# Three small moves in a decoder-layer kernel: late constants, a low weight part behind a scaling, a later first pooling

## The chip, the cores and the metric

The kernel runs on one core of one Trainium2 chip. A core has TensorE (PE: matrix multiplications, with PEld for its weight loads), VectorE (DVE), ScalarE (ACT), GpSimd (POOL) and SyncE (SP), each with its own instruction queue, worked off in order; SP here only issues DMA transfers, and POOL issues the gathers beside its own arithmetic. The metric is the device time of one execution in microseconds (us), lower is better.

## The reference, cut to what is computed

One step of a hybrid layer for a prompt of 512 tokens and 8 sampled tokens, with D = 1024, in float32:

```python
z = rms_norm(x, ln1_g) @ w_in            # u, q, keys and values of three sub-branches, gates
...
cmp_k, cmp_v, end = compress_kv(...)     # the paged cache pooled to one row per 16 tokens
o_c = softmax(q @ cmp_k - alibi) @ cmp_v # compressed blocks
sel = top blocks by the summed weights of o_c, gathered, attended
o_w = sliding window of 512 attended
attn = gates-weighted sum of the three
conv = pointwise(silu(layer_norm(depthwise conv, width 31)))
x = x + (sig(g_conv) * conv + sig(g_attn) * attn) @ w_out
x = x + relu(rms_norm(x) @ w_up)^2 @ w_down, then a last norm
```

The sampled tokens attend to a cache of 2048 tokens in pages of 128, which is read by index; the 16 best blocks of 64 tokens are chosen for each of them.

## The kernel before, in words

All 520 tokens stay on chip, transposed, as a high part hH and a low part hL of 8 slices of 128 channels. A float32 product is made of three products of rounded parts: high by high, low by high, high by low. `dense` (L437, L438, L439, with the accumulators psd) issues them slice by slice for two halves of the tokens, 256 and 264 columns, and remembers the last matmul of each half in the list `ends`. `wload` brings one block of 128 weight columns in two DMA pieces of 256 KB each (tile wraw, three buffers in turn), has ACT round each piece to the high part wh (L414) and lets DVE or POOL subtract to get the low part wl (L416). The first two loads and the seventh on go to POOL, the four between to DVE. SP issues the loads (L402); a load waits until the low part that used its buffer is done.

The start: SP loads the tokens xt (L234), the norm's weights and the first weights. `norm1` goes by a list written out by hand (NORDER): squares on ACT (L330), the root and a Newton step, the scaling of a block of tokens by DVE (L340, kept in the list `scaled`), transposes on PE (L348), high and low parts by ACT (L350) and DVE (L351). Ahead of the first transposes PE multiplies a block of ones by itself 20 times (L356). The first two weight blocks are asked for with `ins=scaled[1]`, which keeps their low parts behind the second scaling in issue order on an engine that has both, and makes no wait.

Then four head groups follow. `project(g)` makes queries, keys and values; for group 0 the queries are `ends[0..3]`, the keys `ends[4]` and `ends[5]`, the values `ends[6]` and `ends[7]`. ACT copies the results out (L569, L587), PE turns them for the outputs (L594, L600). Scores stand in PSUM (L681), DVE adds the distance term and finds the maximum (L645), ACT exponentiates (L649), PE turns the weights (L742) and multiplies by the values (L747). Between them run the pooling of the cache, the convolution's inputs and the taps of the convolution on DVE (L1109).

`pool_cache` gathers the cache's pages by index from POOL (L319, tile cg, four buffers), pools them by matmuls (L775 into psp, then L782) and passes the result through two small layers (L787 to L804). Its first pooling comes, in issue order, behind `ends[P_AT]`. After the last sample (CS_B = 7) it calls `conv_state`, which works on the old convolution rows (L1119 to L1131; PE L1124, DVE L1127 and L1128) and whose last DMA is kept as `UY["cs"]` (L1131). `sample_cmp` chooses the blocks: scores of the samples against the pooled keys (PE L825), a softmax with the table scb (DVE L829), a sum over heads with gsel (PE L837), a ranking with lt (DVE L859 to L863) and a mask spread by eb (PE L869, DVE L870). It begins with the loads of these four tables (L814 to L820).

What stands in the file is not yet the order of the engines. A scheduler lays all instructions out on a simulated timeline by priorities and expected ends, and each engine's queue is what comes out; `tc.issue_after` puts instructions behind another in that layout without a wait, `tc.add_manual_dep` with SYNC makes a real wait. So a constraint at one place can shift rows on all engines for a long stretch.

Of the kernel before, what the change touches and what calls it, by code (L numbers as in the profile page):

```python
# [13 lines left out]
OP = mybir.AluOpType  # L14
# [3 lines left out]
P = 128  # L18
# [41 lines left out]
WIN_E = lambda nc: nc.gpsimd  # L60
XF = False
LOW_D = 6
P_AT = 5
SQ_D, WARM, EARLY = (), 20, 2
NORDER = "q0 q1 s02 m0 m1 t0 t1 q2 q4 q3 s25 m4 m2 t4 m3 t2 t3"
PACK = 5000
# [1 line left out]
SYNC = mybir.DependencyInfo(mybir.DependencyClass.Sync, mybir.DependencyReason.DATA)  # L68
# [62 lines left out]
def hybrid_layer(ctx: ExitStack, tc: tile.TileContext, I, C, O):  # L131
    nc = tc.nc
# [11 lines left out]
    act, dve, pool, pe = nc.scalar, nc.vector, nc.gpsimd, nc.tensor  # L144

    def f32(ap):
        return ap.bitcast(F32)
# [235 lines left out]
    scaled = []  # L383
# [5 lines left out]
    LOW, loaded = [pool], []  # L389
    RAW = [wts, WR_B]  # L390

    def wfetch(w, pieces, r0=0, start=False):
        raws = []
        for h in range(2):
            if start:
                raw = once([P, KD // 2, P], f"wraw{pieces[0][0]}{h}")
            else:
                raw = RAW[0].tile([P, KD // 2, P], F32, name="wraw", tag="raw", bufs=RAW[1])
            o = 0
            for c, n in pieces:  # L400
                r = r0 + D // 2 * h
                nc.sync.dma_start(raw[:, :, o:o + n], w[r:r + D // 2, c:c + n].rearrange("(k p) c -> p k c", p=P))  # L402
                o += n
            raws.append(raw)
        return raws

    def wload(w, pieces, r0=0, low=None, ins=None):
        raws = early.pop(pieces[0][0], None) or wfetch(w, pieces, r0)
        o = sum(n for c, n in pieces)
        wh = wts.tile([P, KD, P], F32R, name="wh")  # L410
        wl = wts.tile([P, KD, P], F32R, name="wl")
        for h, raw in enumerate(raws):
            a, b = wh[:, KD // 2 * h:KD // 2 * h + KD // 2, :o], wl[:, KD // 2 * h:KD // 2 * h + KD // 2, :o]
            act.copy(a, raw[:, :, :o])  # L414
            with after(ins):
                (low or (dve if 2 <= len(loaded) < LOW_D else LOW[0])).tensor_tensor(b, raw[:, :, :o], f32(a), op=OP.subtract)  # L416
        loaded.append(wh)
        return wh, wl

    def after(ins):  # L420
        return tc.issue_after(ins.ins) if ins else nullcontext()

    def packed(makers, *ready_):
        with tc.high_priority(offset=PACK):
            for n, make in enumerate(makers):
                mm = make()
                for i in ready_ if n == 0 else ():
                    tc.add_manual_dep(mm.ins, i.ins.name, SYNC, reason="packed")
        return mm
# [329 lines left out]
    def pool_cache(pp):  # L759
        ps_ = psp if POOL_P else pst  # L760
        for b in range(NB):
# [4 lines left out]
            for rh in range(2):  # L766
                gs, gd = [], []
                for i in range(4):
                    g = pp.tile([P, 2, 512], F32, name="cg", bufs=CG_B)
                    gd.append(gather(cache_c, gic[:, b, i, rh:rh + 1], g))  # L770
                    gs.append(g)
                while len(ends) <= P_AT:
                    yield
                with after(ends[P_AT] if b + rh == 0 else None):
                    packed([lambda r=r, j=j, i=i: pe.matmul(po[32 * i:32 * i + 32, j], wpa[:, 2 * rh + r, j],  # L775
# [34 lines left out]

    def sample_cmp(bp, msk, oC):
        bt = lambda shape, name: bp.tile(shape, F32, name=name)
        gsel = bt([P, 2, 32], "gsel")
        nc.sync.dma_start(gsel, C["gsel"])  # L814
        eb = bt([32, NB, P], "eb")
        nc.sync.dma_start(eb, C["eb"])
        lt, eq, gt = bt([32, 30, 30], "lt"), bt([32, 15, 30], "eq"), bt([32, 15, 30], "gt")
        nc.sync.dma_start(lt, C["lt"])
        scb = bt([P, P], "scb")
        nc.sync.dma_start(scb, C["scb"])  # L820
        pc = bt([P, 2, P], "pcs")
        sv = bt([P, 2, 4], "sv")
        imp = bt([32, P], "imp")
# [32 lines left out]
        for n in (slice(0, 15), slice(15, 30)):  # L856
            a = sc[:, 1][:, None, :].to_broadcast([32, 15, 30])
# [504 lines left out]
    UY = {}  # L1362
# [291 lines left out]
```

## Time and profile before

| | |
|---|---|
| median of 3 runs | 1182.87 us (1182.01 to 1184.0) |
| the profiled execution, its own time | 1182.46 us |
| its span in the trace | 1180.7 us, so 1.76 us lie outside |
| mean granted clock of TensorE | 0.987 |
| PE busy | 1127.9 us, 96% |
| DVE busy | 749.8 us, 64% |
| ACT busy | 544.4 us, 46% |
| POOL busy | 250.4 us, 21% |

The busy shares are means over stages with different limits. In the 40 slices of the span PE is busy nine tenths or more from the fifteenth to the last but one, and seven to nine tenths before. The clock row shows what the throttle granted, 1.00 for the full 2.4 GHz and 0.50 for 1.2 GHz. A row of the timeline gives start, duration, engine, line, operation, output and input tiles and count, then in brackets the idle time before it and what ended it.

### The profile page before, as it was taken

Reading aid. Unit: us, or ns where it says so; the run is one execution under the profiler, and the core shown is the slowest. Engines: PE = TensorE matmul, PEld = TensorE weight load, DVE = VectorE, ACT = ScalarE, POOL = GpSimd, SP = SyncE. Lnnn points to the kernel's source line nnn. Section 1 sums busy time; section 2 is a strip of 40 time slices with the busy share of each in tenths; the row PEclk is TensorE's granted clock in tenths of the full one; section 3 lists DMA queues with packets and bytes.
Section 4 is the critical chain, followed back from the end, with each engine's and each line's share of the span. In section 5 each row is a group of like instructions: output and inputs, shape, how many; then the busy total and the mean of one; then the engine's idle time right before and its main releaser. Section 6 shows DMA issues by size and latency. Waiting matters only on the chain.

```text
span 1180.7 us, 24758 instructions
## 1 busy us (share of the span) xinstructions
PE 1127.9 (96%) x9755; PEld 1001.5 (85%) x9755; DVE 749.8 (64%) x1773; ACT 544.4 (46%) x1384; POOL 250.4 (21%) x284
## 2 busy tenths in 40 slices
PE   7899989899989899999999999999999999999996
PEld 7778867488668475788889889999999999999996
DVE  5441556939999778958959786556543543443476
ACT  5453463543554564566564464344431431432354
POOL 2345445546343122134221000000000000000012
PEclk8999989999999999999999999999999999999998
DMA  6746446428243855688984423333333333333353
GB/s 181 220 132 200 151 134 202 127 75 236 64 130 91 273 194 198 233 303 299 312 282 133 108 63 91 90 93 105 90 90 90 97 97 94 90 90 90 90 175 130
DMA packets 188366, 175.47 MB, mean 149 GB/s; under 512 B 35278, under 2 KB 171022, under 8 KB 182985
## 3 DMA queue, kind: packets, MB, share of 16 engines
q1 hardware_dynamic: 172472, 96.54, 28.6%
q0 software_dynamic: 15296, 76.55, 18.7%
q8 instruction: 77, 1.26, 0.4%
q10 hardware_dynamic: 480, 0.79, 0.2%
q14 instruction: 41, 0.33, 0.1%
HBM read 167.58 MB, written 14.80 MB: 154 GB/s over the span
## 4 chain that ended last, share of the span: by engine, by line
PE 77%; DVE 13%; DMA 3%; ACT 3%; issue 2%; POOL 1%; SPq 0%; DVEq 0%; ACTq 0%; POOLq 0%
PE psd L437 19%; PE psd L438 19%; PE psd L439 19%; DVE y L1109 5%; PE psx L936 3%; PE pss L681 2%; DMA cg<-in_cache_cmp_kv_dram,gic 2%; PE psp L775 2%; PE psy L951 2%; PE pso L747 2%; PE psy L940 2%; PE pst L742 2%; DVE pp L645 1%; DVE pp L731 1%; DVE pt L745 1%
## 5 line engine op out<-in xcount | busy, mean ns | idle before, releaser
L414 ACT CAST wh<-wraw 128x512 fp32r<-128x512 f32 x282 | 161.7, 616 | 289.9 <-PE psd L438 220.0
L437 PE MATMUL psd<-hH,wh 128*128 128x264 f32 (+2 forms) x848 | 249.4, 295 | 0.0
L439 PE MATMUL psd<-hH,wl 128*128 128x264 f32 (+2 forms) x848 | 245.7, 291 | 1.3 <-DVE wl L416 1.3
L438 PE MATMUL psd<-hL,wh 128*128 128x264 f32 (+2 forms) x848 | 245.4, 290 | 0.0
L416 DVE TENSOR_TENSOR wl<-wraw,wh 128x512 fp32r<-128x512 f32 (+1 forms) x230 | 155.4, 711 | 95.0 <-ACT wh L414 90.9
L1109 DVE SCALAR_TENSOR_TENSOR y<-u,cwT,y 128x512 f32<-128x512 f32 x240 | 197.7, 824 | 4.7
L437 PEld LDWEIGHTS psd<-hH,wh 128*128 128x128 f32 (+1 forms) x848 | 159.6, 189 | 8.8 <-issue 5.6
L438 PEld LDWEIGHTS psd<-hL,wh 128*128 128x128 f32 (+1 forms) x848 | 159.9, 189 | 6.6 <-issue 5.9
L439 PEld LDWEIGHTS psd<-hH,wl 128*128 128x128 f32 (+1 forms) x848 | 159.2, 188 | 6.5 <-issue 4.3
L437 PE MATMUL psd<-xgH,wh 128*128 128x264 f32 (+1 forms) x512 | 144.8, 283 | 0.0
L438 PE MATMUL psd<-aT,wh 128*128 128x264 f32 (+1 forms) x512 | 144.7, 283 | 0.0
L437 PE MATMUL psd<-aT,wh 128*128 128x264 f32 (+1 forms) x512 | 144.7, 283 | 0.0
L439 PE MATMUL psd<-aT,wl 128*128 128x264 f32 (+1 forms) x512 | 144.7, 283 | 0.0
L439 PE MATMUL psd<-xgH,wl 128*128 128x264 f32 (+1 forms) x512 | 144.5, 282 | 0.0
L438 PE MATMUL psd<-xgL,wh 128*128 128x264 f32 (+1 forms) x512 | 144.2, 282 | 0.0
L1593 POOL TENSOR_TENSOR attnT<-attnT,gfb 128x512 f32<-128x512 f32 (+1 forms) x8 | 10.5, 1330 | 533.5 <-DVE sqd L1588 533.5
L649 ACT ACTIVATE pp<-pp,st 128x128 f32<-128x128 f32 (+3 forms) x128 | 71.3, 557 | 84.5 <-DVE st L645 84.4
L438 PEld LDWEIGHTS psd<-xgL,wh 128*128 128x128 f32 x512 | 96.6, 189 | 0.0
L439 PEld LDWEIGHTS psd<-xgH,wl 128*128 128x128 f32 x512 | 96.5, 188 | 0.0
L437 PEld LDWEIGHTS psd<-aT,wh 128*128 128x128 f32 x512 | 96.3, 188 | 0.1
L437 PEld LDWEIGHTS psd<-xgH,wh 128*128 128x128 f32 x512 | 96.3, 188 | 0.0
L438 PEld LDWEIGHTS psd<-aT,wh 128*128 128x128 f32 x512 | 96.2, 188 | 0.0
(381 smaller groups left out, 2250.3 us busy)
## 6 DMA issues: line engine op xcount, KB each, us to landing
wraw<-in_w_in_dram SPq DMA_DIRECT2D x88, 256.0 KB, 4.7
wraw<-in_w_down_dram SPq DMA_DIRECT2D x80, 256.0 KB, 2.9
wraw<-in_w_up_dram SPq DMA_DIRECT2D x64, 256.0 KB, 2.9
sg<-in_state_win_kv_dram POOLq DMA_DIRECT2D x8, 1024.0 KB, 5.9
out_dram<-in_state_win_kv_dram SPq DMA_DIRECT2D x8, 1022.0 KB, 18.6
wraw<-in_w_in_dram SPq DMA_DIRECT2D x32, 128.0 KB, 2.6
wraw<-in_w_conv_pw_dram SPq DMA_DIRECT2D x16, 256.0 KB, 2.9
wraw<-in_w_out_dram SPq DMA_DIRECT2D x16, 256.0 KB, 3.1
```

The source lines that it names most:

```text
L414: act.copy(a, raw[:, :, :o])
L416: (low or (dve if 2 <= len(loaded) < LOW_D else LOW[0])).tensor_tensor(b, raw[:, :, :o], f32(a), op=OP.subtract)
L437: pe.matmul(ps[:n], wh[:, k, :n], aH[:, k, c], start=(k == 0), stop=False)
L438: pe.matmul(ps[:n], wh[:, k, :n], aL[:, k, c], start=False, stop=False)
L439: end = pe.matmul(ps[:n], wl[:, k, :n], aH[:, k, c], start=False, stop=(k == KD - 1))
L649: act.activation(ph, ph, AF.Exp, scale=-1.0, bias=st[:, 0, e, i:i + 1], accum_out=st[:, 1, e, i:i + 1])
L681: mms.append(lambda ps=ps, e=e, i=i, xi=xi, nk=nk: pe.matmul(ps, rq(e, i), KR[g, e, r][:, 32 - xi:32 + nk], start=True, stop=True))
L742: pe.transpose(ps[:, o:o + P], phs[e][i][:, P * j:P * j + P], ident)
L747: packed([lambda j=j, e=e: pe.matmul(po[64 * e:64 * e + 64, P * j:], vt[:, j, r], pts[e][:, off[j]:off[j] + P * (4 - j)], start=(r == 0 an ...
L775: packed([lambda r=r, j=j, i=i: pe.matmul(po[32 * i:32 * i + 32, j], wpa[:, 2 * rh + r, j], gs[i][:, r, 256 * j:256 * j + 256], start=(rh ...
L936: pe.transpose(ps[:, r], g[:, r, P * h:P * h + P], ident)
L1109: prev = dve.scalar_tensor_tensor(yk, u[:, w:w + NP_], cwT[:, k, w:w + 1], yk, op0=OP.mult, op1=OP.add)
```

## The change

It does three things. `P_AT` goes from 5 to 7, so that the first pooling stands behind the values' last matmul instead of the keys'. In `wload`, the first half's low part of a load with `ins` gets a real wait for the second scaling. And the loads of the four tables of `sample_cmp` are put behind `UY["cs"]` in issue order, and come as lt, scb, gsel, eb.

```diff
-P_AT = 5
+P_AT = 7
...
             act.copy(a, raw[:, :, :o])
             with after(ins):
-                (low or (dve if 2 <= len(loaded) < LOW_D else LOW[0])).tensor_tensor(b, raw[:, :, :o], f32(a), op=OP.subtract)
+                lo = (low or (dve if 2 <= len(loaded) < LOW_D else LOW[0])).tensor_tensor(b, raw[:, :, :o], f32(a), op=OP.subtract)
+            if ins and h == 0:
+                tc.add_manual_dep(lo.ins, ins.ins.name, SYNC, reason="scaled")
         loaded.append(wh)
...
     def sample_cmp(bp, msk, oC):
         bt = lambda shape, name: bp.tile(shape, F32, name=name)
+        hold_ = tc.issue_after(UY["cs"].ins)
+        hold_.__enter__()
+        lt, eq, gt = bt([32, 30, 30], "lt"), bt([32, 15, 30], "eq"), bt([32, 15, 30], "gt")
+        nc.sync.dma_start(lt, C["lt"])
+        scb = bt([P, P], "scb")
+        nc.sync.dma_start(scb, C["scb"])
         gsel = bt([P, 2, 32], "gsel")
         nc.sync.dma_start(gsel, C["gsel"])
         eb = bt([32, NB, P], "eb")
         nc.sync.dma_start(eb, C["eb"])
-        lt, eq, gt = bt([32, 30, 30], "lt"), bt([32, 15, 30], "eq"), bt([32, 15, 30], "gt")
-        nc.sync.dma_start(lt, C["lt"])
-        scb = bt([P, P], "scb")
-        nc.sync.dma_start(scb, C["scb"])
+        hold_.__exit__(None, None, None)
```

The same instructions stand on each engine in both programs, but not in the same order. From the file's line 416 on, the line numbers of the new program are 2 higher, behind the tables' loads 5 higher: L439, L440, L441 there are L437, L438, L439 here, L596 is L594, L647 is L645, L777 is L775, L1132 is L1127.

SP, the front of the queue, before:

```order
1 L814 DMA gsel_4937<-c_gsel_dram 128x64
2 L816 DMA eb_4939<-c_eb_dram 32x1024
3 L818 DMA lt_4941<-c_lt_dram 32x900
4 L820 DMA scb_4945<-c_scb_dram 128x128
5 L234 DMA xt0_89<-in_x_prompt_dram 128x1024
6 L234 DMA xt1_90<-in_x_prompt_dram 128x1024
7 L237 DMA g1b_94<-in_ln1_g_dram 128x1024
8 L234 DMA xt4_93<-in_x_sample_dram 8x1024
```

and in the change:

```order
1 L234 DMA xt0_89<-in_x_prompt_dram 128x1024
2 L234 DMA xt1_90<-in_x_prompt_dram 128x1024
3 L237 DMA g1b_94<-in_ln1_g_dram 128x1024
4 L234 DMA xt4_93<-in_x_sample_dram 8x1024
5 L239 DMA ident_95<-c_ident_dram 128x136
```

The four tables are gone from here and stand behind L1131's DMA, ahead of the window copies (L1380).

PE, the end of group 0's keys (psd rows of 128x264), before; psd rows of 128x256 that follow are the values:

```order
150 L437 MATMUL psd<-hH,wh 128x264
151 L438 MATMUL psd<-hL,wh 128x264
152 L439 MATMUL psd<-hH,wl 128x264
153 L775 MATMUL psp<-cg,wpa 32x256 x16
154 L594 MATMUL psj<-ident,qkv 128x128 x2
155 L437 MATMUL psd<-hH,wh 128x256
156 L438 MATMUL psd<-hL,wh 128x256
```

and in the change, at the same place and where the pooling now stands:

```order
152 L441 MATMUL psd<-hH,wl 128x264
153 L596 MATMUL psj<-ident,qkv 128x128 x2
154 L439 MATMUL psd<-hH,wh 128x256
155 L440 MATMUL psd<-hL,wh 128x256
...
206 L440 MATMUL psd<-hL,wh 128x256
207 L441 MATMUL psd<-hH,wl 128x256
208 L777 MATMUL psp<-cg,wpa 32x256 x2
209 L683 MATMUL pss<-qkv 128x384
210 L683 MATMUL pss<-ks,qkv 128x384
211 L777 MATMUL psp<-cg,wpa 32x256 x14
```

The pooling went from row 153 to rows 208 to 211, and the turning of the queries took its place. On POOL the two low parts of the first weight block changed places: the second half's comes first, the first half's, which has the new wait, second. From there to about 400 us every pooling stands 50 to 90 rows later on PE than before. In the stretch that ran from 310 to 335 us, 8 to 11 more conv taps (L1109) stand on DVE ahead of the same head's scores (L645); some 15 scores later the count is the same again.

DVE, the last pair of 128x512 scores (L645 with dist; "ISA st" reads the maximum) and the softmax of the block choice, before:

```order
742 L829 ISA pcs,sv<-psp,scb 128x128
743 L829 ISA sv 128x1
744 L745 COPY pt<-pst 128x512
745 L655 TENSOR_SCALAR st<-st 128x8
746 L656 RECIPROCAL st<-st 128x8
747 L645 ISA pp,st<-pss,dist 128x512
748 L645 ISA st 128x1
749 L657 TENSOR_TENSOR st<-st,gtok 128x8
750 L645 ISA pp,st<-pss,dist 128x512
751 L645 ISA st 128x1
752 L832 TENSOR_SCALAR sv<-sv 128x2
```

and in the change:

```order
739 L647 ISA pp,st<-pss,dist 128x512
740 L647 ISA st 128x1
741 L658 RECIPROCAL st<-st 128x8
742 L416 TENSOR_TENSOR wl<-wraw,wh 128x512
743 L1073 SCALAR_TENSOR_TENSOR u<-tb,ah 128x264
744 L747 COPY pt<-pst 128x384
745 L659 TENSOR_TENSOR st<-st,gtok 128x8
746 L1132 TENSOR_TENSOR tm<-psp,cwT 128x480
747 L657 TENSOR_SCALAR st<-st 128x8
748 L719 TENSOR_TENSOR pc<-pc,st 128x128 x2
749 L1133 TENSOR_REDUCE ys<-tm 128x4x4
750 L658 RECIPROCAL st<-st 128x8
```

A second low part stands between the two scores (row 738), another pair L1132 and L1133 at rows 752 and 754, and the two L834 (L829 before) at rows 759 and 761; before, all of these stood ahead of the pair. On PE 16 rows of L825 and two groups of L1124 come behind the last scores that stood ahead of them. From about 470 us on all engines have the same order in both programs.

## Rows read from the trace of the kernel before

**Rows 1.** Timeline, SP, the front of its queue: start, duration, engine, line.

```profile
0.75 0.40 SPq L814 DMA_DIRECT2D gsel<-c_gsel_dram  x1
...
2.60 0.91 SPq L234 DMA_DIRECT2D xt<-in_x_prompt_dram  x2
```

**Rows 2.** Timeline, start, ACT, DVE and PE; in brackets idle time and its releaser.

```profile
6.84 1.06 ACT L330 ACTIVATE sq<-xt 128x1024 f32<-128x1024 f32 x1 [4.59 <-DMA xt<-in_x_prompt_dram]
...
12.09 1.09 PE L348 MATMUL pst<-ident,xt 128*128 128x128 f32 x8 [3.42 <-DVE xt L340]
...
15.46 0.59 ACT L350 CAST hH<-pss 128x512 fp32r<-128x512 f32 x1 [0.32 <-PE pss L348]
...
16.31 0.59 ACT L350 CAST hH<-pss 128x512 fp32r<-128x512 f32 x1 [0.27 <-PE pss L348]
...
16.82 0.58 PE L438 MATMUL psd<-hL,wh 128*128 128x256 f32 x1
...
23.91 0.28 PE L438 MATMUL psd<-hL,wh 128*128 128x256 f32 x1
...
24.03 0.28 PE L439 MATMUL psd<-hH,wl 128*128 128x256 f32 x1
...
24.91 0.19 DVE L351 TENSOR_TENSOR hL<-pst,hH 128x32 fp32r<-128x32 f32 x1 [0.65 <-ACT hH L350]
...
26.59 1.09 PE L348 MATMUL pss<-ident,xt 128*128 128x128 f32 x8 [0.35 <-DVE xt L340]
```

**Rows 3.** Busy time by stretch: length, PE, PEld, DVE, ACT, POOL, clock, DMA share, GB/s.

```profile
14.00:16.00 2.00, 1.69 (x8) 1.57 (x8) 1.54 (x3) 1.68 (x4) 2.00 (x2) 0.50 1.00 356
...
46.00:48.00 2.00, 2.00 (x24) 1.00 (x20) 1.38 (x5) 1.44 (x4) 0.00 (x0) 0.50 0.26 70
...
300.00:350.00 50.00, 45.12 (x353) 31.48 (x353) 47.10 (x121) 25.08 (x87) 20.39 (x25) 1.00 0.36 106
```

**Rows 4.** One line's instructions, L340: shortest, median and longest in ns.

```profile
L340 DVE SCALAR_TENSOR_TENSOR xt<-xt,rs,g1b x5: 1267/1276/2306, 10.7 to 25.3; 128x1024 f32<-128x1024 f32 x4, 8x1024 f32<-8x1024 f32 x1
```

**Rows 5.** Timeline, end of group 0's keys and the first pooling.

```profile
41.40 0.28 PE L439 MATMUL psd<-hH,wl 128*128 128x264 f32 x1
...
42.72 0.62 ACT L414 CAST wh<-wraw 128x512 fp32r<-128x512 f32 x1 [5.98 <-DMA wraw<-in_w_in_dram]
43.36 0.37 ACT L587 COPY qkv<-psd 128x256 f32<-128x256 f32 x1
...
45.04 3.43 PE L775 MATMUL psp<-cg,wpa 128*32 128x256 f32 x32 [3.35 <-DMA cg<-in_cache_cmp_kv_dram,gic]
```

**Rows 6.** Chain of waits around 395 us: start, duration, what.

```profile
395.33 1.93 PE psp L775 x32
```

**Rows 7.** What PE waits for: total us, times, longest us.

```profile
PE psp L787 <- ACT acc L784: 3.0, 1, 3.0
```

**Rows 8.** Timeline, SP, late in the attention.

```profile
398.13 0.79 SPq L1131 DMA_DIRECT2D out_dram<-in_state_conv_dram  x1
```

**Rows 9.** Timeline around the block choice, DVE and PE.

```profile
445.40 0.58 PE L1124 MATMUL psp<-ident,sr 120*128 120x120 f32 x4
...
447.50 0.64 DVE L1127 TENSOR_TENSOR tm<-psp,cwT 128x480 f32<-128x480 f32 x1
...
448.18 0.65 DVE L1128 TENSOR_REDUCE ys<-tm 128x16 f32<-128x480 f32 x1
...
450.09 1.08 PE L825 MATMUL psp<-compK,Qz 128*32 128x128 f32 x32
...
451.30 0.69 DVE L416 TENSOR_TENSOR wl<-wraw,wh 128x512 fp32r<-128x512 f32 x1
...
451.91 0.42 DVE L1068 SCALAR_TENSOR_TENSOR u<-tb,ah 128x264 f32<-128x264 f32 x1
...
452.84 0.28 DVE L829 CUSTOM_DVE_ANT_0 pcs<-psp,scb 128x128 f32<-128x128 f32 x1
```

**Rows 10.** One line's instructions, L1109 (conv taps): shortest, median and longest in ns.

```profile
L1109 DVE SCALAR_TENSOR_TENSOR y<-u,cwT,y x240: 729/752/3399, 194.2 to 647.2; 128x512 f32<-128x512 f32 x120
```

## The prediction

> **What bounds the kernel now.** I read the table of engines and the row of the granted clock first, then the list of what TensorE (PE) waits for, then the timeline around each long wait, and last the instruction orders of both programs. PE is busy for nearly the whole span, and the orders of the two programs are the same, row for row, from about 470 us on, so this change can only earn or lose before that, where PE waits. The start waits for one load: the activation engine (ACT) begins its first square at 6.84, after 4.59 us idle for xt [rows 2], and that load is issued at 2.60, behind four constant loads that begin at 0.75 [rows 1]. PE then stands 3.42 us until the first scaled block is there [rows 2], and its clock is at half level when it goes on [rows 3]. The next long wait is the first cache pooling: PE stands 3.35 us for a gather, and its 32 pieces then take 3.43 us [rows 5], with the clock at half [rows 3]; the same 32 pieces take 1.93 us later on [rows 6]. In 300 to 350 us PE is busy 45.12 and VectorE (DVE) 47.10 of 50 us [rows 3]: there DVE is the nearer bound, and a DVE order that is worse costs.
>
> The sum is made against the profiled execution, 1182.46 us, which is 0.41 under the median of the runs, 1182.87. Some 0.2%, or 2.4 us, is what a measurement of this kernel can tell from no change.
>
> **The constants, off the front of SP's queue: -1.85 us.** SP issues gsel, eb, lt and scb at 0.75 to 2.55 and xt at 2.60 [rows 1]; in the change xt is the first row of the queue. 2.60 - 0.75 = 1.85, and squares, scalings and transposes hang on that load. It could give less if the landing were held by something else; the 4.59 us of ACT's wait [rows 2] name only the load, so I take all of it, with 0 as the other end. The four loads now stand behind row L1131, issued at 398.13 [rows 8]; they are first wanted at 452.84 [rows 9]. Four issues at the pitch of 0.46 us that they had [rows 1] add some 1.9 us to SP 50 us before anybody reads them: 0, and without that cover 1.9 us at most. Issue early and wait late, so that the fixed cost lies beside work, is a rule of the Trainium skill ("DMA: Bandwidth & Descriptors", Rules for kernel authors); it speaks against loading late. By it this part would earn nothing, and the sum would be 1.85 us higher, 1181.5. The trace agrees with it only where nothing more urgent stands behind the load.
>
> **What the earlier start brings besides: -0.9.** PE's gap of 3.42 us shrinks by 1.85 to some 1.6, since the warm-up matmuls end when they did. Idle stretches of 3.4 us are followed by a lower clock in this trace, so I expect the full level to hold. Before, the 46 matmuls from 16.82 to 24.03 took 7.2 us; at the 0.12 us between 23.91 and 24.03 they take 5.5 [rows 2]. Not all of that reaches the chain: what it frees is ACT's two waits for transposes, 0.32 and 0.27, and the 0.65 that DVE waited at 24.91 for a cast behind PE [rows 2]. The three sum to 1.24, the far end; the near end is 0, if the clock falls as before. I take 0.9, near the far end, as the gap halves. DVE has no other long wait from there to 37 us, and it makes the gather indices and frees the weight buffers, so gathers and weights move ahead with it.
>
> **The first low part behind the second scaling: 0.** The second scaling took 2306 ns where the others took 1276 [rows 4], 1.03 longer, beside a low part on GpSimd (POOL). In the new order the other half of that weight comes first on POOL, and the half that waits comes second; nothing else on POOL waits for them before the gathers, whose indices come much later. PE needs the first low part not before 16.82 [rows 2]. A faster scaling helps ACT's transposes only by the 0.32 and 0.27 that are counted already, because the casts in front of them on ACT wait for weights. So 0; it cannot give more than 0.32, and it costs something only if PE's first L439 became late: four low parts at up to 2.25 us would have to slip by over 1 us. VectorE and GpSimd hold a shared SBUF port pair by turns, for a whole instruction, when a VectorE operation has two SBUF inputs (the Trainium skill, "SBUF — State Buffer", SBUF: two separate sides). By that rule the 1.03 us would go whole, and the sum would be 1178.6 if all of it reached the end; the row's 1.03 agrees with the rule, but ACT's waits say that little of it gets through.
>
> **The first pooling behind the values' projection: -2.8.** In the old order PE's queue stands at L775 from 41.69 to 45.04 with other work behind it, part of which could run [rows 5]. In the new one the next row is the query transpose L594 (now L596), which wants ACT's copy L587. That copy ends at 43.73, behind the cast of 42.72 that waited for a weight load [rows 5]. So the gap becomes 43.73 - 41.69, some 2.05, and 1.3 us are won. The bounds are 0 and 3.35. The pooling comes some 50 rows later with all gathers landed, and at full clock its 32 pieces take 1.93 in place of 3.43 [rows 5, 6]: 1.5 more, or 0 if the clock still falls after the shorter gap. The gathers of the second pooling wait for these matmuls to free their buffers, and start later; they have the rest of the first head group as cover.
>
> **The middle, re-dealt: 0.** Pooling groups lag by 50 to 90 rows on PE up to 400 us and the scheduler deals DVE's and ACT's rows anew around them. The largest single wait there is L787 for ACT's acc, 3.0 us [rows 7]; it can go or double, so -3.0 and +3.0. I can't sign it and take 0.
>
> **The block choice's tail: +2.7.** Behind the last pair of 128x512 scores DVE now has two low parts (0.69 each), one L1068 (0.42), two L1127 (0.64), two L1128 (0.65) and the pair L829 (0.28 each), which stood ahead of them [rows 9]: 1.38 + 0.42 + 1.28 + 1.30 + 0.56 = 4.9 us. PE has L825, 1.08, and two groups of L1124, 0.58 each, behind instead of ahead [rows 9], 2.2 us of cover. The chain L829, L837, L838 to L866, L869 then ends 4.9 - 2.2 = 2.7 later against PE's other work. Ends: 0, if PE and DVE arrive early enough for the slack to absorb it, and 4.9.
>
> **Sum:** -1.85 - 0.9 + 0 - 2.8 + 0 + 2.7 = -2.85, so 1182.46 - 2.85 = **1179.6 us**.
>
> **Rivals.** *The tail costs nothing* (0.25): PE and DVE keep the early gain and the choice's chain finds slack. For it: neither engine is busy all the time there. Against: the constants' consumers stand later on both. It gives 1182.46 - 5.55 = 1176.9, and 1173.9 if the 3.0 us wait goes as well.
>
> *The clock eats the start* (0.20): the new gaps of 1.6 and 2.05 us still bring the half level. Then the 0.9 and the 1.5 fall away: -1.85 - 1.3 + 2.7 = -0.45, 1182.0. Against it: both falls of the clock in the rows here follow idle times of over 3.3 us.
>
> *DVE's conv taps stand ahead of a head's scores* (0.20), the slower side. At 310 to 335 us the new order puts 8 to 11 more conv taps (L1109) ahead of a head's scores, 7.9 us of DVE work at some 0.75 each [rows 10], while PE has only 2.4 us more of its own rows to do in the meantime. Where DVE is busy 47.10 of 50 us [rows 3] the difference, 5.5, shows as PE idle time and is not regained: -2.85 + 5.5 = +2.65, 1185.1. It decides against the forecast once PE's idle time in that stretch grows by over 2.85 us. Against it: the order catches up within the next 15 scores, so PE can use what it did not do earlier.
>
> **How the numbers follow.** The forecast has 0.35, mostly between 1178.2 and 1181.2; of this 0.24 lies under the 1180.5 from which it counts as faster, 0.11 above. The tail rival adds 0.25 to faster, the clock rival 0.20 to no change, the conv rival 0.19 to slower and 0.01 to no change. Sum: faster 0.49, same 0.32, slower 0.19. The range goes from 1174.0 (tail free, most of the 3.0 us wait gone) to 1185.1 (conv rival); what is left out is worse than that on DVE, or more of the middle.
>
> **What would show it.** The first square at some 5.0 instead of 6.84; the clock at full from 12 to 20; PE's first block transpose some 1.85 earlier; the second scaling near 1.28; a gap of some 2 us ahead of L596 and none ahead of the first L777; L777's first 32 pieces in 1.9; the first psx matmuls behind L874 (L869 before) some 3 us earlier than before. The forecast is wrong if that point is later than now, if the clock still falls twice in the first 50 us, or if PE's busy time in 300 to 350 falls clearly under 45.12.

## The result: slower, and the loss sits in three places

The change takes 1191.53 us in the median of 10 runs (1188.76 to 1197.7). The kernel before, run beside it, takes 1184.25 (1182.01 to 1187.24). The ratio is 1.0071 [1.0056, 1.0086]: slower by 8.4 us, where 1179.6 was forecast, and above the range. The profiled execution of the change took 1197.41 us, one of its longest, and that of before 1182.46, one of its shortest: the profiles stand 14.95 us apart, the medians 7.3 here and 11.9 in a second batch (e8, the change run once more). Ratios therefore carry the verdicts below, and profiles tell only where a stretch lies; where the same stretch differed between profiles, the text gives the range.

The engines and the granted clock of the change, from its page:

```profile
span 1195.6 us, 24769 instructions
...
PE 1135.0 (95%) x9755; PEld 1005.9 (84%) x9755; DVE 748.8 (63%) x1773; ACT 543.2 (45%) x1384; POOL 245.3 (21%) x284
...
PEclk9899899999999999899999999999999999999998
```

PE does the same 9755 matmuls and is busy 7.1 us longer than before (1127.9), at a mean granted clock of 0.981 against 0.987. So about half of the 14.95 us between the two profiles is PE working at a lower clock, and the rest is PE standing.

**The start came as forecast in this execution, but not in every one.** The timeline of the change (start, duration, engine, line; in brackets idle time and its releaser), from the front of SP's queue to PE's first block:

```profile
0.75 0.88 SPq L234 DMA_DIRECT2D xt<-in_x_prompt_dram  x2
...
4.35 1.06 ACT L330 ACTIVATE sq<-xt 128x1024 f32<-128x1024 f32 x1 [2.10 <-DMA xt<-in_x_prompt_dram]
...
9.66 1.09 PE L348 MATMUL pst<-ident,xt 128*128 128x128 f32 x8 [1.54 <-DVE xt L340]
```

And the instructions of its line L340 (shortest, median and longest in ns):

```profile
L340 DVE SCALAR_TENSOR_TENSOR xt<-xt,rs,g1b x5: 1264/1273/1286, 8.3 to 21.6; 128x1024 f32<-128x1024 f32 x4, 8x1024 f32<-8x1024 f32 x1
```

The first square starts 2.49 us earlier and the first block's transposes 2.43 earlier [rows 2]; the longest scaling is 1286 ns where it was 2306 [rows 4]. The same stretch as in [rows 3], with two more (length, PE, PEld, DVE, ACT, POOL, clock, DMA share, GB/s), shows the clock at the full level ahead of 20 us:

```profile
14.00:16.00 2.00, 1.56 (x13) 1.36 (x12) 1.18 (x2) 1.97 (x4) 1.65 (x2) 1.00 0.17 46
16.00:18.00 2.00, 2.00 (x19) 2.00 (x18) 0.17 (x1) 1.71 (x5) 0.00 (x0) 1.00 0.10 35
18.00:20.00 2.00, 2.00 (x19) 2.00 (x19) 1.81 (x6) 0.00 (x0) 0.00 (x0) 1.00 0.04 12
```

The last block's transposes then start at 22.9 instead of 26.59: 3.7 us earlier. The second profile of the same kernel (e8) shows another start, by its timeline of PE and its stretch:

```profile
9.69 1.09 PE L348 MATMUL pst<-ident,xt 128*128 128x128 f32 x8 [2.52 <-DVE xt L340]
...
12.00:14.00 2.00, 0.99 (x5) 0.59 (x4) 1.14 (x2) 2.00 (x5) 2.00 (x2) 0.50 0.96 341
```

The first transposes come at the same time, but the warm-up matmuls end at 7.17 instead of 8.12, so the gap is longer, and the half level lasts from 10.9 to 17.7. Fourteen of the profiles here have the tables loaded late and so the early start. In five of them the gap is 1.13 to 1.66 us, the full level holds to 20, and the last block starts at 22.8 to 23.3. In the other nine the gap is 1.83 to 2.55 us, half level follows (in four from 10.8 to 11.3 us on, in five from 15.1 to 15.7), and the last block starts at 23.9 to 24.5.

Then the gain is lost again, and more. What PE waits for in the change (total us, times, longest us):

```profile
PE pso L749 <- DVE pt L747: 8.5, 11, 1.6
PE psj L596 <- ACT qkv L589: 5.6, 1, 5.6
PE psp L802 <- DVE hidc L799: 4.7, 1, 4.7
PE pss L683 <- DVE st L647: 4.3, 7, 1.3
PE psp L874 <- issue: 3.6, 1, 3.6
PE psp L777 <- DMA cg<-in_cache_cmp_kv_dram,gic: 3.6, 2, 2.9
```

The stop ahead of L802 was not in the prediction at all. At L874 there was no stop before: L869 stood behind PE's other work and started at 469.75. The stop ahead of L596 was forecast with 2.05 us. (L681 of before is L683 here, L797 is L799, L800 is L802, L869 is L874 and L1109 is L1114.)

**The first stop, ahead of L596.** The timeline of the change on PE, ACT and POOL:

```profile
30.82 1.15 POOL L319 DMA_INDIRECT cg<-in_cache_cmp_kv_dram,gic  x1 [15.16 <-DVE gic L372]
...
38.83 0.28 PE L441 MATMUL psd<-hH,wl 128*128 128x264 f32 x1
...
43.62 0.62 ACT L414 CAST wh<-wraw 128x512 fp32r<-128x512 f32 x1 [10.53 <-DMA wraw<-in_w_in_dram]
44.26 0.37 ACT L589 COPY qkv<-psd 128x256 f32<-128x256 f32 x1
...
44.69 0.69 PE L596 MATMUL psj<-ident,qkv 128*128 128x128 f32 x2 [5.57 <-ACT qkv L589]
```

PE finishes the keys 2.6 us earlier than before (38.83 against 41.40 [rows 5]), but the cast that holds ACT's queue starts 0.9 us later (43.62 against 42.72): it waits for a weight piece that loads beside the cache gathers. The clock is at half behind the stop:

```profile
46.00:48.00 2.00, 2.00 (x12) 2.00 (x11) 0.33 (x2) 0.07 (x1) 0.00 (x0) 0.50 0.99 260
48.00:50.00 2.00, 2.00 (x11) 2.00 (x11) 0.00 (x0) 0.00 (x0) 0.00 (x0) 0.50 0.49 133
```

By the first L602 (L600 before), at 51.6, the change is 2.1 us behind, and the 32 pooling pieces, which before has done by then, still lie ahead of it: the gain of the start is gone. How long this stop is differs: five profiles with this order so far have 5.57 (the change), 5.14 (e8), 4.06 (e13), 3.10 (e7) and 2.93 us (e6), so the one shown is the longest. The moved pooling itself does what it should: it starts without a wait, and its second group of 32 pieces takes 1.93 in one piece at 70.56, as in [rows 6].

**The second stop, ahead of L802.** The chain of waits around 118 us in the change (start, duration, what):

```profile
118.34 12.43 DMA out_dram<-tok
...
130.84 0.43 DVE hidc L799
...
131.31 1.22 PE psp L802 x2
```

And the timeline of DVE, POOL and SP there:

```profile
115.12 0.36 SPq L497 DMA_DIRECT2D out_dram<-tok  x1
...
117.79 1.27 SPq L497 DMA_DIRECT2D out_dram<-tok  x2
...
115.83 0.95 POOL L319 DMA_INDIRECT cg<-in_cache_cmp_kv_dram,gic  x1
...
119.57 1.43 POOL L319 DMA_INDIRECT cg<-in_cache_cmp_kv_dram,gic  x1 [0.30 <-PE psp L789]
...
130.24 0.69 DVE L508 TENSOR_TENSOR ptmp<-attnT,wc 128x512 f32<-128x512 f32 x1 [10.05 <-DMA out_dram<-tok]
```

A store of the prompt's tokens (L497) takes 12.43 us. DVE's L508, which writes a buffer that this store still reads, stands 10.05 us, and in its queue behind it stands the L799 that PE wants. PE works at half level from 128.9 to 135.7. Beside the stores the fifth batch of cache gathers is under way, issued from 115.83 on. In before the same batch was issued earlier than the stores, and its DVE waited 1.59 us there, behind another 3.75 that the profile puts down to a weight load:

```profile
107.25 0.95 POOL L319 DMA_INDIRECT cg<-in_cache_cmp_kv_dram,gic  x1 [1.33 <-PE psp L775]
...
111.00 0.94 POOL L319 DMA_INDIRECT cg<-in_cache_cmp_kv_dram,gic  x1 [0.30 <-issue]
...
115.30 0.36 SPq L495 DMA_DIRECT2D out_dram<-tok  x1
...
122.82 3.19 DVE L506 TENSOR_TENSOR ptmp<-attnT,wc 128x512 f32<-128x512 f32 x2 [1.59 <-DMA out_dram<-tok]
```

The gathers take buffers that a pooling frees, so a pooling 50 to 90 rows later puts them later too: on top of the stores.

**The third stop, ahead of L874.** The timeline of DVE and PE in the change:

```profile
477.04 1.07 PE L851 MATMUL psp<-compV,pcT 128*32 128x256 f32 x16
...
481.48 0.17 DVE L871 TENSOR_SCALAR m<-sc 32x30 f32<-32x30 f32 x1
...
481.75 3.59 PE L874 MATMUL psp<-m,eb 32*128 32x32 f32 x16 [3.65 <-issue]
```

And its busy time by stretch:

```profile
481.00:485.00 4.00, 3.25 (x16) 3.28 (x16) 0.62 (x2) 0.00 (x0) 0.00 (x0) 0.50 1.01 427
485.00:490.00 5.00, 5.00 (x48) 4.44 (x48) 4.59 (x10) 0.59 (x1) 0.00 (x0) 0.50 1.00 423
490.00:495.00 5.00, 4.74 (x32) 2.71 (x31) 4.82 (x9) 3.41 (x7) 0.00 (x0) 0.93 0.08 33
```

PE's queue stands at L874 until DVE has the block choice's mask (L871, done at 481.65), so the wait is DVE's although the row says issue. The 16 matmuls then take 3.59 us, where they took 1.97 in before, and the half level lasts to 490. L874 starts 12.0 us later than L869 did, and the end is 14.9 us later.

### The profile page after: what moved, and what is told of

Read it like the earlier page. It is cut to its first block, busy times and chain, and to the rows that moved or that the text cites. A ratio compares the mean times of both kernels' runs of the same rounds, so it can differ in the third digit from the quotient of the medians.

```text
span 1195.6 us, 24769 instructions
## 1 busy us (share of the span) xinstructions
PE 1135.0 (95%) x9755; PEld 1005.9 (84%) x9755; DVE 748.8 (63%) x1773; ACT 543.2 (45%) x1384; POOL 245.3 (21%) x284
## 4 chain that ended last, share of the span: by engine, by line
PE 77%; DVE 12%; DMA 5%; issue 2%; ACT 2%; SPq 1%; POOL 0%; DVEq 0%; ACTq 0%; POOLq 0%
PE psd L441 19%; PE psd L439 19%; PE psd L440 19%; DVE y L1114 5%; PE psx L941 3%; PE pss L683 3%; PE psp L777 3%; PE pso L749 2%; PE pst L744 2%; DMA cg<-in_cache_cmp_kv_dram,gic 2%; PE psy L956 2%; PE psy L945 2%; DVE pp L733 1%; DVE pp L647 1%; DMA out_dram<-tok 1%
## 5 line engine op out<-in xcount | busy, mean ns | idle before, releaser
L439 PE MATMUL psd<-hH,wh 128*128 128x256 f32 (+2 forms) x848 | 250.4, 296 | 2.5 <-ACT hH L350 1.7
L441 PE MATMUL psd<-hH,wl 128*128 128x256 f32 (+2 forms) x848 | 247.7, 294 | 3.3 <-DVE wl L416 2.4
L440 PE MATMUL psd<-hL,wh 128*128 128x256 f32 (+2 forms) x848 | 246.7, 291 | 0.4 <-DVE hL L351 0.4
L1114 DVE SCALAR_TENSOR_TENSOR y<-u,cwT,y 128x512 f32<-128x512 f32 x240 | 201.8, 841 | 4.8
L439 PEld LDWEIGHTS psd<-hH,wh 128*128 128x128 f32 (+1 forms) x848 | 161.5, 191 | 10.6 <-issue 5.3
L441 PEld LDWEIGHTS psd<-hH,wl 128*128 128x128 f32 (+1 forms) x848 | 160.7, 190 | 9.7 <-issue 5.0
L440 PEld LDWEIGHTS psd<-hL,wh 128*128 128x128 f32 (+1 forms) x848 | 161.5, 190 | 5.0 <-issue 3.8
L439 PE MATMUL psd<-xgH,wh 128*128 128x264 f32 (+1 forms) x512 | 144.8, 283 | 0.0
L440 PE MATMUL psd<-aT,wh 128*128 128x264 f32 (+1 forms) x512 | 144.7, 283 | 0.0
L439 PE MATMUL psd<-aT,wh 128*128 128x264 f32 (+1 forms) x512 | 144.7, 283 | 0.0
L441 PE MATMUL psd<-aT,wl 128*128 128x264 f32 (+1 forms) x512 | 144.7, 283 | 0.0
L441 PE MATMUL psd<-xgH,wl 128*128 128x264 f32 (+1 forms) x512 | 144.5, 282 | 0.0
L440 PE MATMUL psd<-xgL,wh 128*128 128x264 f32 (+1 forms) x512 | 144.2, 282 | 0.0
L440 PEld LDWEIGHTS psd<-xgL,wh 128*128 128x128 f32 x512 | 96.6, 189 | 0.0
L441 PEld LDWEIGHTS psd<-xgH,wl 128*128 128x128 f32 x512 | 96.5, 188 | 0.0
L439 PEld LDWEIGHTS psd<-aT,wh 128*128 128x128 f32 x512 | 96.3, 188 | 0.1
L439 PEld LDWEIGHTS psd<-xgH,wh 128*128 128x128 f32 x512 | 96.3, 188 | 0.0
L440 PEld LDWEIGHTS psd<-aT,wh 128*128 128x128 f32 x512 | 96.2, 188 | 0.0
```

The source lines that it names most:

```text
L439: pe.matmul(ps[:n], wh[:, k, :n], aH[:, k, c], start=(k == 0), stop=False)
L440: pe.matmul(ps[:n], wh[:, k, :n], aL[:, k, c], start=False, stop=False)
L441: end = pe.matmul(ps[:n], wl[:, k, :n], aH[:, k, c], start=False, stop=(k == KD - 1))
L1114: prev = dve.scalar_tensor_tensor(yk, u[:, w:w + NP_], cwT[:, k, w:w + 1], yk, op0=OP.mult, op1=OP.add)
```

## The experiments

The ratio is to the kernel before, run beside it on the same chip. Five batches of runs were made (e1 to e4, e5 to e8, e9 to e12, e13 to e16, e17 and e18).

**Which part loses? (e1 to e4)** Each part of the diff alone, and the two small ones together. e1 is the line `P_AT`, e2 the tables, e3 the wait of the low part, e4 both of these.

> Only the first pooling is moved behind the values' projection (P_AT 7); tables and low part as before. Theory A (the loss is the moved pooling: a longer stop of TensorE ahead of the turned queries, its clock at half afterwards, and the gathers of later poolings running beside weight loads and output stores): slower by 8 to 14 us, since the gain of the start is not there either; the tables' matmul L869 some 10 us later than before. Theory B (the loss is the tables: with their loads late the block choice or the earlier start lose): within 3 us of the kernel before.

> Only the four tables are loaded late; pooling and low part as before, and the order of the queues is the old one between the start and the block choice. Theory A: faster by 1 to 4 us, the start 2 to 3.5 us ahead at the first turned block and at least half of that kept to the end. Theory B: slower by 3 us or more, with a wait ahead of the table matmuls. A third, that the start's gain is always swallowed by the first weights that arrive beside the gathers: within 1 us of before.

> Only the low part of the first half waits for the second scaling. All theories: within 1 us of before; the second scaling near 1.3 instead of 2.3 us, and 0 to 0.6 us earlier transposes of the second block.

> The change without the moved pooling. Theory A: faster than before by 2 to 5 us, and faster than the change by 8 to 13; the start 3.5 us ahead at the transposes of the last block. Theory B: as slow as the change, 5 to 9 us over before.

e1 took 1199.22 us, 1.0115 [1.0097, 1.0133]; e2 1186.16, 1.0001 [0.9987, 1.0016]; e3 1185.25, 0.9999 [0.9984, 1.0014]; e4 1186.88, 1.0008 [0.9993, 1.0022]. The moved pooling alone makes the whole loss. e1 even lies above the change (1.0071, and 1.0095 in e8), so the two small parts may give something in the new order; no batch holds both, and it is not shown. In the old order they give nothing that can be measured, against the 1 to 5 us that theory A expected of e2 and e4, though the start of e2 runs 3.6 us earlier by the last block. What PE waits for in e1, whose order is nearly that of the change:

```profile
PE psj L594 <- ACT qkv L587: 4.8, 1, 4.8
...
PE psp L800 <- DVE hidc L797: 4.2, 1, 4.2
PE psp L869 <- DVE m L866: 3.7, 1, 3.7
```

The same three stops, without either small part.

**The first stop: gathers held back (e5).** The first gather waits for the cast that PE's queue hangs on; the order stays that of the change:

```diff
+                    if b + rh + i == 0:
+                        tc.add_manual_dep(gd[0].ins, casts[3].ins.name, SYNC, reason="gather")
```

> The change, with the first gathers of the cache waiting for the cast of the values' second weight piece, so that this piece is no longer loaded beside them; the order of all rows but one small gather is that of the change. Theory C (early losses count: the 5.6 us stop ahead of L596 and the 4.7 us stop at L802 go through to the end): the stop ahead of L596 falls to 2 us or less, and the time falls by 3 to 6 us, to 1185 to 1189. Theory D (the early losses are taken up by waits near 200 us, and the loss comes from poolings that are late in the second half and from the block choice behind them): the stop goes, the time stays within 2 us of the change.

1193.29 us, 1.0067 [1.0053, 1.0080], beside 1.0095 [1.0079, 1.0110] for the change in the same batch (e8). The stop is gone; a shorter one appears at the pooling, by the timeline of PE in e5:

```profile
39.60 0.44 PE L597 MATMUL psj<-ident,qkv 128*128 128x128 f32 x2 [0.39 <-ACT qkv L590]
...
50.35 0.62 PE L782 MATMUL psp<-cg,wpa 128*32 128x256 f32 x4 [2.20 <-DMA cg<-in_cache_cmp_kv_dram,gic]
```

L597 (L596 of the change) waits 0.39 instead of 5.57 and 5.14, so the gathers beside the weight load were what held the cast: in the six runs that hold them it starts 3.9 to 4.7 us after the piece was issued, in all others 6.4 to 10.1. The worth is 0.0028 x 1184, some 3.3 us, with intervals that just touch. The same edit was not tried in before.

**The second stop: no token stores (e6).** The four stores at L497 are left out:

```diff
-            if t < 4:
-                nc.sync.dma_start(o_cmp_p[0, 0, P * t:P * t + P].rearrange("t j h d -> t (j h d)"), tok)
-            else:
+            if t == 4:
```

> The change without the four stores of the compressed branch's prompt rows (L497), which are left out; the order of all other rows is that of the change. TensorE's 4.7 us stop at L802 (VectorE held at L506 by a store that ran beside gathers) should go under both theories. Theory C: the time falls by 4 to 7 us. Theory D: by 2 us at most, and the lag is the same as the change's from about 230 us on.

1190.82 us, 1.0036 [1.0017, 1.0056] beside the 1.0095 of e8: 0.59%, some 7 us. The wait at L802 is gone from its list, and the one at L872 (L874 of the change) stands unaltered:

```profile
PE psp L872 <- issue: 3.6, 1, 3.6
...
PE psj L594 <- ACT qkv L587: 2.9, 1, 2.9
```

The shorter first stop is not the edit's doing: nothing ahead of it was altered.

**The choice brought forward, and the change once more (e7, e8).** `W_P` is the pace at which the order lets the cache pooling go ahead; 65 instead of 55 deals the middle anew:

```diff
-W_P, W_D, W_S, W_D2, W_C, W_U = 55, 55, 120, 40, 300, 20
+W_P, W_D, W_S, W_D2, W_C, W_U = 65, 55, 120, 40, 300, 20
```

> The change with the pooling's share in the interleaving of the generators at 65 instead of 55: the order is the change's up to the fifth pooling group, and behind it the poolings come earlier, the block choice's mask matmul before the last head's end instead of behind it. Theory C: the early stops are all there, so no better than the change by more than 2 us. Theory D: the stop of 3.7 us ahead of L869's counterpart and the half clock behind it go, and the time falls by 5 to 12 us, to 1180 to 1187.

> The change itself beside the other three: 1189 to 1198, as before; it sets the level that the three are compared with.

e7 took 1184.41 us (1179.74 to 1194.8, the widest spread here), 1.0000 [0.9979, 1.0021]; e8 1197.45, 1.0095 [1.0079, 1.0110]. The mask's matmuls in e7 (shortest, median and longest in ns, then first and last start):

```profile
L874 PE MATMUL psp<-m,eb x16: 271/271/292, 444.7 to 448.4; 32*128 32x32 f32 x16
```

With these matmuls at 444.7 instead of 481.8 us the third stop is gone, and with it the whole loss, although a 4.0 us stop ahead of L802 is still there. This asks whether a stop that comes early costs anything once the choice comes early.

**Is 65 a better pace in itself? (e9 to e12)** e9 is e5 with two buffers of its own for DVE's `ptmp`, e10 is before, e11 is before with tables and low part, e12 is e5, all at 65. The buffer in e9:

```diff
-                    tmp = temp("ptmp")[:, :NP_].rearrange("p (c w) -> p c w", w=16)
+                    tmp = ap.tile([P, NP_], F32, name="ptmp", tag="ptmp", bufs=2).rearrange("p (c w) -> p c w", w=16)
```

> The change with three repairs: the first gathers held as in e5, the compressed branch's products (L506) in two buffers of their own so that VectorE no longer waits for a token store, and the pooling paced at 65. If the three losses add (early stop 3 to 4, store collision 6 to 7, late block choice 5 to 6 us), it is faster than the kernel before by 4 to 10 us, 1176 to 1182. If each repair only opens the next wait, it is within 3 us of before, as e7 is.

> The kernel before with the pooling paced at 65 and nothing else. If e7 came back to the time of before only because its pace suits any of these kernels, this is faster than before by 6 us or more. If the pace only repairs what the moved pooling made late, it is within 3 us of before.

> The tables late and the low part's wait, first pooling where it was, paced at 65. Beside e10 it says what these two parts bring where the block choice is done early: 2 us less than e10 if the start's gain is kept, the same as e10 within 1.5 if it is lost again further on, as e4 had it.

> e7 with the first gathers held; the order of e7's rows but for one small gather. If the early stop's loss goes through to the end here as in e5: 3 to 4 us less than e7's 1184.4, so 1180 to 1182. If it is taken up where the choice is no longer at the end: within 1.5 us of e7.

e9 took 1192.37 us, 1.0060 [1.0044, 1.0076]; e10 1217.03, 1.0272 [1.0253, 1.0291]; e11 1220.42, 1.0297 [1.0279, 1.0315]; e12 1185.80, 1.0013 [1.0001, 1.0025]. The pace that repairs the change costs before 32 us. What PE waits for in e10 names one new place:

```profile
PE pst L742 <- ACT tok L596: 12.5, 1, 12.5
```

It is a stop of the second kind: by its timeline ACT's L596 starts at 402.06, released by a transfer into the output (out_dram<-in_state_win_kv_dram), and PE's transposes stand behind it from 390.2 to 402.7. e9 dealt its order anew as well, so it doesn't tell what the buffers do. e11's list has the stop of e10 too, with 7.4 us; why e9 and e11 lose as much as they do was not followed further. e12 gives nothing over e7: its first stop is gone and the time is no better, so with the choice early nothing shows that this stop alone costs anything.

**The third stop, and all three (e13 to e16).** The ranking behind the mask runs over half of the blocks only, in the change (e13) and in before (e16); e14 puts this together with the edits of e5 and e6; e15 is before without the token stores.

```diff
-        for n in (slice(0, 15), slice(15, 30)):
+        for n in (slice(0, 15),):
```

> The change with only the first 15 of the 30 blocks ranked in the choice (one pass of L859 to L863's counterparts is left out, some 3.3 us of VectorE); rows up to the mask matmul as in the change. If the choice at the end holds the path there: the 3.65 us stop ahead of the mask matmul falls to under 1, the half clock behind it goes or shrinks, and the time falls by 3 to 6 us, to 1.004 to 1.007 of before. If something else holds that place: less than 1 us.

> The change with the first gathers held, without the four token stores (left out) and with half the ranking (left out). If the three losses are separate and add, 4 + 6.6 + 4 us: 1182 to 1185, that is 0.997 to 1.000 of before. If the rest of the re-dealt order costs by itself: 1.003 or more.

> The kernel before without the four token stores (left out), the order of all other rows unchanged. If these stores cost only where gathers run beside them: within 1.5 us of before. If they cost in any order: 4 us or more below before, and e6 says nothing of the moved pooling.

> The kernel before with half the ranking (left out), as e13. Here the mask matmul and the last head end together, so a chain shorter by 3.3 us should bring 0 to 2 us. If it brings as much as e13, the choice is no more on the path in the change than before.

e13 took 1188.97 us, 1.0040 [1.0023, 1.0056]; e14 1182.00, 0.9976 [0.9963, 0.9989]; e15 1183.90, 0.9998 [0.9985, 1.0010]; e16 1186.07, 1.0011 [0.9998, 1.0023]. The timeline of PE in e13 around the mask's matmuls:

```profile
474.82 1.07 PE L851 MATMUL psp<-compV,pcT 128*32 128x256 f32 x16
476.64 1.94 PE L874 MATMUL psp<-m,eb 32*128 32x32 f32 x16 [0.75 <-ACT oC L854]
```

0.75 us of waiting instead of 3.65, and 1.94 instead of 3.59 for the matmuls: the full level holds there, and half level comes only from 479.3 to 486.1, where the change had it from 480.5 to 490.7. The change did not run in this batch; against its 1.0071 and 1.0095 in others the stop is worth 3.7 to 6.5 us. In before neither leaving out the stores nor halving the ranking gains anything, so these two gains in the change are not those of work left out. e14 is faster than before, with an interval that lies below 1: with the three stops out the whole loss is gone, and some 2.8 us are won. That these come from the earlier start is likely, but no run shows it by itself.

**A complete kernel without the stops (e17, e18).** The first gathers are held as in e5; the fifth batch waits for the last token store; e18 has the pace of 65 besides:

```diff
+                    if (b, rh, i) == (2, 0, 0) and len(stores) > 3:
+                        tc.add_manual_dep(gd[0].ins, stores[3].ins.name, SYNC, reason="stores")
```

> The change, complete, with the first gathers held as in e5 and the fifth batch of gathers (beside which the four token stores ran) waiting for the last of these stores; the order is the change's but for a few rows of VectorE and ScalarE. If it is the running side by side that makes the stores late, the stop at L802 falls under 2 us and the time to about e5 and e6 together, 1185 to 1188 (1.000 to 1.003 of before). If the late gathers hold up POOL's low parts behind them instead: no better than e5, 1.006.

> The same with the pooling paced at 65 as in e7, so that the block choice is done early. If the early and the late losses are separate, it is the fastest here: 1177 to 1182, 0.994 to 0.998 of before. If the early loss is taken up by the end, as in e12: within 2 us of before.

The chain of waits around 113 us in e17:

```profile
113.04 6.74 DMA out_dram<-tok
```

The last token store lands 6.74 us after its issue, without the fifth batch beside it, where the change's took 12.43: the gathers made about half of that time, and what made the rest is open. DVE then waits 3.23 and 1.39 us where it waited 10.05, and PE's waits for it at this line (L809) come to 1.2 us in the whole run. e17 took 1187.25 us, 1.0021 [1.0007, 1.0035], with the third stop still in it (3.6 us at L881). e18 took 1179.88 (1178.66 to 1180.96), 0.9956 [0.9940, 0.9972], where before took 1184.76 beside it: faster than both kernels, by 0.44% against before. What PE waits for in e18:

```profile
PE psp L784 <- DMA cg<-in_cache_cmp_kv_dram,gic: 7.2, 5, 2.6
PE pst L745 <- DVE news L605: 3.3, 2, 2.7
PE pss L684 <- DVE st L648: 3.3, 6, 0.8
PE pso L750 <- DVE pt L748: 2.7, 5, 0.9
```

None of the three stops is left; no wait in this list is longer than 2.7 us. e12, with the first gathers held and the same pace, had 1.0013 in its own batch; what e18 has besides is the fifth batch behind the stores.

## Why the prediction was wrong

The sum went wrong at two terms, the first pooling and the middle, and a third, the tail, was too small. Of the three signs by which the forecast would be wrong, two came in the profile of the change: the psx matmuls behind L874 are later than before, and PE's busy time in 300 to 350 us fell. The third, that the clock falls twice in the first 50 us, did not come there and did in e8. By its steps:

- **The constants, -1.85: held in the profile, not in the time.** The first square starts 2.49 us earlier, and the first block 2.43: the load was issued 1.85 earlier and was also used sooner, 3.60 us after its issue instead of 4.24. Alone, in e2, it gives 1.0001 [0.9987, 1.0016]. In the profiles of e2 and e4 1.6 us of the gain are left at 50 us. That of e4 is 2.3 to 2.9 us ahead from 190 to 470 us and loses 1.6 of it by 481, behind a stretch of half level at 469.7 to 476.5; one profile doesn't explain a median, so why the early start doesn't show there stays open. In e14, with the stops gone, the time lies below that of before. The rule weighed against this term, issue early and wait late (the Trainium skill, "DMA: Bandwidth & Descriptors", Rules for kernel authors), gave 0 for it; e2's ratio agrees with 0, and the rows at the start do not.
- **The earlier start, -0.9: it held in some executions, by luck in the one profiled.** In the change's profile the full level held from 12 to 20 us behind a gap of 1.54, and the gain at the last block was 3.7 against 2.75 forecast. But the premise that the warm-up matmuls end when they did is wrong: they end at 8.12 in this profile, 8.66 in before's, and at 7.1 to 8.4 in the fourteen with the early start. In nine of these the half level came, and the gain at the last block was 2.1 to 2.7. So the clock rival was right at the start more often than not. At the next place, behind the stop at 44.69, the half level came behind a gap of 5.57 and not the 2.05 that the rival spoke of.
- **The low part, 0: right.** The second scaling lost its 1.03 us, as by the port rule (the Trainium skill, "SBUF — State Buffer", SBUF: two separate sides), and e3's 0.9999 shows that none of it reached the end. In e2, which has the late tables without the wait, the longest scaling is 1285 ns as well, and POOL's four low parts take 5.96 us there where they take 5.15 in the change: with the early start it was POOL that was slower.
- **The first pooling, -2.8: wrong in sign.** The step that failed is "So the gap becomes 43.73 - 41.69, some 2.05". It kept the release where it had been and forgot that the keys would end earlier by the start's own gain, and that gathers and weight load would move together. The gap was 5.57 in this profile and 2.93 to 5.14 in four others, not 2.05, and the half level came behind it in four of the five. The worth of taking it out is some 3.3 us (e5). That the pooling itself would run without a wait and at full clock was right.
- **The middle, 0 (±3.0): the main miss.** "I can't sign it and take 0" looked at the largest wait that was there and not at what the gathers would now meet. The note under the first pooling, that the gathers of a later pooling start later, had its cover wrong: they meet the token stores, whose slow landing holds DVE, then PE. e6 puts that at some 7 us, more than twice the bound of 3.0 that I gave.
- **The tail, +2.7: right sign and place, too small.** The stop is 3.65 us. The half level that follows costs 1.6 us at L874 alone and lasts to 490.7; by e13 the whole is 3.7 to 6.5 us. I had priced the wait and not the clock behind it.
- **The conv-tap rival** had the right side and the wrong place. PE's busy time from 300 to 350 us did fall, from 45.12 to 43.62, and its own price hung on 2.85 us more idle time there; e14 wins everything back with the same order in this stretch.

The sum of the three (3.3 + 7 + 3.7 to 6.5, that is 14 to 17 us) stands beside the 11 to 14 us between the change (1.0071 to 1.0095) and e14 (0.9976). They add up within their intervals, which are some 3 to 5 us wide each; so the theory that early stops are taken up again further on fell for the second stop, as far as this order goes, and for the first as far as e5's touching intervals carry. In the order with pace 65 the first stop's worth does not show (e7 against e12).

## What to carry to other kernels

A row moved on the busiest engine also moves whatever waits for the buffers that it frees: list the transfers it releases, and the other transfers that will be under way at the new time, above all stores whose source buffer an in-order engine is about to write. An earlier start is worth only what the next fixed release leaves of it, so put the new start time into every later gap before subtracting; and price a stop of some 3 us with the half-clock stretch that may follow it. Before a stretch of one profile is called the change's doing, look at the same stretch in a second profile of the same kernel. A constant that sets an order (5 against 7, 55 against 65) belongs to one order: re-tune it after a move, and put an explicit wait between two transfers that must not meet.

## What the hardware showed that was not expected

- Transfers on SP's queue took about one and a half to two times as long beside gathers. The second piece of the values' weights was issued at 33.73 us, 2.9 behind the first gather, and its cast began 9.9 us later; in before the issue was at 36.30, also 2.9 behind the first gather, and the cast 6.4 later. With the gathers held back (e5) it was issued at 33.83 and the cast began 4.7 us later. Five profiles of the change's order gave 7.3 to 9.9 us, so what sets the time within that range stays open. The last token store took 12.43 us beside the gathers and 6.74 without the fifth batch beside it (e17).
- Stops are not always followed by the half level, and their length alone does not tell. At the start gaps of 1.13 to 1.66 us were not followed by it, and gaps of 1.83 to 2.55 were. But ahead of L596 a stop of 3.10 (e7) left the full level, one of 2.93 (e6) did not; before's profile has a gap of 1.95 near 393 us with the full level behind it, while in e3, with the same order, one of 2.25 there had the half level from 396 on. Up to some 490 us PE spent some 20 us at half level in before's profile and 34 in the change's, and the runs of each kernel spread by 0.4 to 0.8%.
